# Order of the first loads, placement of the w_up casts, and the last down group and adds in a fused decoder layer

## The chip, the cores and the metric

The kernel runs on the 8 cores of one Trainium2 chip, each with its own part of the tokens. A time is device microseconds of the slowest core; the fast executions of one kernel differ by some 1 to 4 us. A second, slow state, with one die at a lower clock, appears now and then in any program on eight cores: here some executions of the kernel before (890 to 964 us) and of four variants (846 to 980 us).

Each execution also gives the span of every core. Their mean over the eight cores scatters by only about 0.3 us from one execution to the next (standard deviation), and it is used here beside the time, under the name **mean span**.

## The reference, cut to what matters

One decoder layer over 2,064 prompt positions for each of 8 sequences and 128 single tokens; widths 1,024 and 2,816.

```python
h = rmsnorm(x, g_pre_mix)
u, v, bg, cg, ga, gb = split(h @ w_in)             # w_in: 1024 x 4096
a = multiscale_pool(u, ..., w_pool, pool_scale)
b = (bg * causal_dwconv(cg * v)) @ w_conv_out
x = x + rmsnorm((sigmoid(ga) * a + sigmoid(gb) * b) @ w_o, g_post_mix)
h = rmsnorm(x, g_pre_ffn)
gate, val = split(causal_dwconv(h @ w_up))         # w_up: 1024 x 5632, as 44 blocks
y = (silu(gate) * val) @ w_down                    # 22 rows of blocks, 8 output groups
x = x + rmsnorm(y, g_post_ffn)
```

## The kernel before

Each core holds activations with channels on the 128 partitions. The mixer (up to the `w_o` product) runs over five token tiles of 512 or 392 columns, the FFN over six tiles of 344. Weights come as float32 and are cast to bf16 by the DMA on their way in; GpSimd issues these casts, and also the DMA that adds to its destination (`acc=True`). All instructions are first collected, then a list scheduler in the build fixes each engine's order. Loads can be tied to a point of the program by `after=[last_pe[0]]`: they are issued after that TensorE group.

TensorE's groups keep their order, except the short sums of the norms, which float: such a sum is placed when it has been ready for a set time (the patience, in nanoseconds) or when TensorE would stand still.

```python
# in the scheduler, for TensorE: c is the next fixed group, f the next floating sum
if c is None or ready[f.idx] + max(400.0, min(f.flt, f.pri - s - 4000.0)) <= s or sf <= s - 200.0:
    c, s = f, sf
```

The head. `xs0` are the five loads of the first x tile; SyncE issues them.

```python
wload(W_IN, w_in, 0)
warm(60)                                   # 60 small matmuls on a constant
for i in range(1, 16):
    wload(W_IN, w_in, i, after=[last_pe[0] if i < 3 else xs0[1]])
...                                        # w_pool, rest of w_in, w_co, then x1: after=[xs0[1]]
```

The 44 casts of `w_up` (256 KB in SBUF, 0.262 MB each) and the residual of tile 3, which accumulating transfers add:

```python
for i in range(16):                        # first half of the last mixer tile, L = 4
    F_block(L, i)
    wup(1)
    if i == 4:
        WO(L - 1)
        epi(L - 1)                         # tile 3: multiply, pool_dma(r, xs, acc=True), square, sums
...
for m in range(8):                         # second half: gates
    merge(t, m, *g[m])
    if t == L:
        wup(1)
...                                        # then one per w_o group, and one per FFN pair j of tile 0
if (t, j) in ((0, 9), (0, 11), ...):       # the 8 casts of w_down, from FFN pair 9 on
    wdn()
```

The end. A down group `m` is one chain of 22 matmuls over the gated rows `gb`; the last tile's eight groups follow the last pair directly. Then the norm, a multiply per row pair and the residual:

```python
pe([(bank(b, NB), wb[:, k, :], gb.ap[:, k, :]) for k in range(FC)], [W_DN.t(m, 1), gb.t()], [("ps", b)], NB)
...
steps = ((0, 2, None, "acc"), (2, 2, None, "pool"), (4, 2, 0, "dve"), (6, 2, 2, "dve"))
#         first row, rows, PSUM bank, who adds the residual: accumulating DMA, GpSimd, VectorE
```

## Time and profile before

| | kernel before |
|---|---|
| time, median before the change was tried | 822.18 us |
| profiled execution: cores | 817.4 to 820.1 us |
| mean span, 30 fast executions | 818.34 us |
| slowest core, mean of the same | 819.95 us |
| last matmul's start to the end, mean of 8 cores | 11.63 us |

The prediction below shows the page's first part, the waits of core 0 and its stall near 320 us. In these lines PE is TensorE, DVE VectorE, ACT ScalarE, POOL GpSimd and SP SyncE; L469 is the line of the kernel in which a helper issues every matmul. Core 0 is not typical, as only its clock fell after that stall, so here are core 1's stretches of TensorE from the timeline: start, duration, instruction group and count, and in brackets the idle time before the stretch and what the profile says ended it.

```profile
43.61 274.32 PE L469 MATMUL ps<-big 128*128 128x392 bf16 x1581 [0.54 <-DVE big L658]
319.42 6.13 PE L469 MATMUL ps<-big 128*128 128x392 bf16 x36 [1.49 <-DVE big L509]
326.08 80.32 PE L469 MATMUL ps<-big 128*128 128x392 bf16 x537 [0.52 <-ACT big L700]
407.26 371.37 PE L469 MATMUL ps<-big 128*128 128x346 bf16 x2536 [0.86 <-DVE big L821]
...
806.19 0.31 PE L469 MATMUL ps<-big 128*128 128x344 bf16 x1 [0.32 <-ACT big L848]
```

After 43.61 us TensorE stands still five times (the one left out here is the 0.69 us at 779 that the prediction discusses). Together that is 1.49 + 0.52 + 0.86 + 0.69 + 0.32 = 3.9 us in 763; everything else to be won lies before 43.61 and after 806.19.

The issue-to-landing view of the stretch from 285 to 420 us, core 0 (count, KB, median us from issue to landing):

```profile
big<-w_up POOLq DMA_DIRECT2D x38, 256.0 KB, 10.3
...
big<-xT POOLq DMA_DIRECT2D x4, 392.0 KB, 13.6
```

The last line is the four accumulates of tile 3.

### The profile page before, as it was taken

To read this page: it belongs to the slowest core of one execution; us is meant where nothing else is said; L and a number is where in the kernel's file an instruction comes from. 1 tells how busy PE (TensorE), PEld (TensorE's weight loads), DVE (VectorE), ACT (ScalarE), POOL (GpSimd) and SP (SyncE) were. 2 spreads that over 40 slices of the span, in tenths; PEclk is the share of its full clock that TensorE was granted. 3 is DMA by queue.
4 is the path that set the end of the run, shared out by engine and by line. 5 is a ranking of instruction groups with operands and counts; after the bars stand their busy time and mean duration, and the time that the engine had idled before them with its cause. 6 is when DMAs were issued, how large, how long until landed. Compare 5 with 4: busy or idle time off the path is not lost.

```text
span 820.1 us, 16719 instructions; the slowest of 8 cores (817.4 to 820.1 us)
## 1 busy us (share of the span) xinstructions
PE 798.2 (97%) x5118; PEld 498.9 (61%) x5118; DVE 563.4 (69%) x1054; ACT 450.7 (55%) x903; POOL 259.9 (32%) x296
## 2 busy tenths in 40 slices
PE   7999999999999998999999999999999999999994
PEld 5454455555555554666666666666666666666662
DVE  3896547877977595588986486568566765785722
ACT  3533375676475544686754475456556555765532
POOL 6542002002101261499532252225222522242221
PEclk9999999999999999999999999999999999999998
DMA  9999706567117799999960132015101500040063
GB/s 182 201 160 156 152 20 136 148 164 157 41 36 158 109 171 208 169 159 171 183 113 1 35 46 53 1 36 70 36 2 36 70 2 1 6 66 2 1 133 77
DMA packets 63735, 75.18 MB, mean 92 GB/s; under 512 B 3072, under 2 KB 59264, under 8 KB 63632
## 3 DMA queue, kind: packets, MB, share of 16 engines
q0 software_dynamic: 41440, 44.97, 38.9%
q1 hardware_dynamic: 22208, 29.14, 12.8%
q8 instruction: 44, 0.72, 0.3%
q14 instruction: 43, 0.35, 0.2%
HBM read 81.53 MB, written 22.90 MB: 127 GB/s over the span
## 4 chain that ended last, share of the span: by engine, by line
PE 90%; DMA 4%; DVE 2%; issue 2%; POOL 1%; ACT 1%; DVEq 0%; ACTq 0%; POOLq 0%
PE ps L469 90%; DMA big<-xT 4%; POOL big L482 1%; DVE big L549 0%; DVE big L783 0%; DVE big L821 0%; ACT big L520 0%; DVE big L509 0%; DVEq L1078 0%; DVE big L578 0%; ACT L520 0%; DVE big L658 0%; DVE big L867 0%; ACT big L848 0%; ACT big L768 0%
## 5 line engine op out<-in xcount | busy, mean ns | idle before, releaser
L469 PE MATMUL ps<-big 128*128 128x346 bf16 (+5 forms) x5118 | 798.2, 319 | 10.6 <-POOL big L922 2.9
L469 PEld LDWEIGHTS ps<-big 128*128 128x128 bf16 x5118 | 498.9, 98 | 309.6 <-issue 15.8
L821 DVE SCALAR_TENSOR_TENSOR big<-ps,big 128x344 f32<-128x344 f32 (+1 forms) x528 | 281.1, 569 | 94.8 <-ACT big L817 74.9
L835 POOL TENSOR_TENSOR big<-big 128x344 bf16<-128x344 f32 x132 | 125.5, 952 | 258.5 <-DVE big L821 186.2
L817 ACT ACTIVATE big<-ps,big 128x344 f32<-128x344 f32 (+1 forms) x264 | 139.4, 541 | 67.5 <-PE ps L469 61.7
L834 ACT ACTIVATE big<-big 128x344 f32<-128x344 f32 x132 | 64.6, 489 | 47.9 <-DVE big L821 45.9
L700 ACT ACTIVATE big<-ps 128x392 f32<-128x392 f32 (+1 forms) x80 | 38.9, 512 | 51.8 <-PE ps L469 34.7
L480 POOL DMA_DIRECT2D big<-xT x16 | 15.8, 997 | 153.4 <-DVE big L713 147.0
L845 ACT ACTIVATE big<-ps,big 128x344 f32<-128x344 f32 x48 | 26.0, 546 | 58.8 <-PE ps L469 55.8
L482 POOL DMA_DIRECT2D big<-w_up x44 | 33.3, 758 | 64.6 <-PE ps L469 52.8
L713 DVE SCALAR_TENSOR_TENSOR big<-ps,big 128x392 f32<-128x392 f32 (+1 forms) x40 | 25.8, 645 | 33.7 <-PE ps L469 31.4
L509 DVE TENSOR_TENSOR big<-big 128x1568 bf16<-128x1568 bf16 (+3 forms) x28 | 24.5, 875 | 32.2 <-ACT big L732 26.0
L851 DVE TENSOR_TENSOR big<-big 128x688 bf16<-128x688 bf16 x17 | 8.8, 518 | 41.5 <-ACT big L848 41.5
L480 POOL DMA_DIRECT2D yT<-big x21 | 27.3, 1523 | 31.0 <-DVE big L867 17.3
L730 ACT ACTIVATE big<-ps,big 128x392 f32<-128x392 f32 (+1 forms) x40 | 24.5, 613 | 13.0 <-PE ps L469 12.9
L606 DVE TENSOR_TENSOR big<-big 128x406 f32<-128x406 f32 (+7 forms) x50 | 29.8, 598 | 1.5 <-ACT big L628 0.2
L482 POOL DMA_DIRECT2D big<-w_in x32 | 23.2, 743 | 20.6 <-DMA big<-w_in 10.9
L575 ACT ACTIVATE big<-big 128x392 f32<-128x392 f32 (+1 forms) x20 | 12.7, 638 | 30.6 <-DVE big L664 30.5
L768 ACT ACTIVATE big<-big 128x784 bf16<-128x784 f32 (+1 forms) x20 | 17.8, 891 | 18.5 <-DMA big<-xT 16.0
L578 DVE SCALAR_TENSOR_TENSOR big<-big 128x392 f32<-128x392 f32 (+1 forms) x40 | 25.5, 644 | 3.6 <-ACT big L575 3.0
L848 ACT ACTIVATE big<-ps 128x344 bf16<-128x344 f32 x48 | 21.6, 451 | 10.4 <-PE ps L469 10.2
L719 DVE TENSOR_TENSOR big<-big 128x392 bf16<-128x392 f32 (+1 forms) x40 | 24.9, 631 | 2.3
(62 smaller groups left out, 353.4 us busy)
## 6 DMA issues: line engine op xcount, KB each, us to landing
big<-w_up POOLq DMA_DIRECT2D x44, 256.0 KB, 10.0
big<-w_in POOLq DMA_DIRECT2D x32, 256.0 KB, 22.6
yT<-big POOLq DMA_DIRECT2D x21, 344.0 KB, 6.2
big<-xT POOLq DMA_DIRECT2D x16, 392.0 KB, 8.9
yT<-big SPq DMA_DIRECT2D x8, 784.0 KB, 8.5
big<-w_dn POOLq DMA_DIRECT2D x8, 704.0 KB, 14.1
big<-xT SPq DMA_DIRECT2D x6, 784.0 KB, 6.2
big<-h2T SPq DMA_DIRECT2D x6, 692.0 KB, 5.8
```

The source lines that it names most:

```text
L469: ins = e.matmul(o, lhsT=l, rhs=x, start=(start and i == 0), stop=(stop and i == last))
L480: return S.add("pool", lambda e: e.dma_start(out=out, in_=in_, accum_op=ALU.add, max_dma_last_dim=mx), r, w, dma=True, byts=byts, pri=pri, ...
L482: return S.add("pool", lambda e: e.dma_start(out=out, in_=in_, max_dma_last_dim=mx), r, w, dma=True, byts=byts, pri=pri, after=after)
L578: dve(lambda e, k=k: e.scalar_tensor_tensor(out=cv, in0=p[:, 2 + k + lo:2 + k + N], scalar=cc(C_WC + 4 * k + c), in1=cv, op0=ALU.mult, op1 ...
L606: dve(lambda e, nx=nx, cur=cur, s=s, a2=a2: e.tensor_tensor(out=nx[:, a2:W], in0=cur[:, a2:W], in1=cur[:, a2 - s:W - s], op=ALU.add), [ct] ...
L700: act(lambda e, b=b, g=g: e.activation(out=GT[t].ap[:, g, lo:N], in_=bank(b, N, lo), func=AF.Sigmoid), [("ps", b)], [GT[t].t(g, 1)], N, ps ...
L713: dve(lambda e: e.scalar_tensor_tensor(out=A_, in0=bank(bp, N, lo), scalar=cc(C_PS + m), in1=A_, op0=ALU.mult, op1=ALU.mult), [("ps", bp), ...
L817: act(lambda e, b=b, fj=fj, tt=tt: e.activation(out=tt[:, 0:n], in_=bank(b, n), func=AF.Copy, scale=cc(C_WF + fj)), [("ps", b), KCST], [to ...
L821: dve(lambda e, b=b, fj=fj, tt=tt, k=k: e.scalar_tensor_tensor(out=tt[:, 0:n], in0=ps[:, b * 512 + k:b * 512 + k + n], scalar=cc(C_WF + 44 ...
L834: act(lambda e: e.activation(out=g, in_=g, func=AF.Silu), [T.t(0, 1)], [T.t(0, 1)], NB, tab="silu")
L835: S.add("pool", lambda e: e.tensor_tensor(out=gb.ap[:, j, :], in0=g, in1=v, op=ALU.mult), [T.t()], [gb.t(j, 1)], dur=NB * 2.17 + 100)
L845: act(lambda e: e.activation(out=Y.ap[:, m, :], in_=bank(b, NB), func=AF.Copy, scale=cc(C_G4 + m)), [("ps", b), KCST], [Y.t(m, 1)], NB, ps ...
```

## The change

The intent, part by part: (1) the first x tile is to come in alone before any weight; (2) fewer `w_up` casts are to stand before and among the accumulates, and the rest goes out two per gate pair; (3) floating sums wait longer for a natural gap, and the eight multiplies of `epi_x` are spread; (4) the first down group of the last tile is cut, so that it can start before the last two gated rows exist; (5) no accumulating DMA at the end: GpSimd adds rows 0 to 2, VectorE adds rows 3 to 7 from PSUM.

```diff
-  ... ready[f.idx] + max(400.0, min(f.flt, f.pri - s - 4000.0)) <= s ...
+  ... ready[f.idx] + max(1000.0, min(f.flt, f.pri - s - 4000.0)) <= s ...
@@ the down groups
-        pe([... for k in range(FC)], [W_DN.t(m, 1), gb.t()], [("ps", b)], NB)
+        for k0, k1 in ((0, 20), (20, 21), (21, 22)) if t == NTB - 1 and m == 0 else ((0, FC),):
+            pe([... for k in range(k0, k1)], [W_DN.t(m, 1), gb.t(k0, k1 - k0)],
+               [("ps", b)], NB, start=k0 == 0, stop=k1 == FC)
@@ the last adds
-            steps = ((0, 2, None, "acc"), (2, 2, None, "pool"), (4, 2, 0, "dve"), (6, 2, 2, "dve"))
+            steps = ((0, 2, None, "pool"), (2, 1, None, "pool"), (4, 2, 0, "dve"), (6, 2, 2, "dve"), (3, 1, 4, "dve"))
@@ the head
-    wload(W_IN, w_in, 0)
     warm(60)
-    for i in range(1, 16):
-        wload(W_IN, w_in, i, after=[last_pe[0] if i < 3 else xs0[1]])
+    for i in range(16):
+        wload(W_IN, w_in, i, after=[xs0[1 if i else 0]])
@@ the casts
             if t == L:
-                wup(1)
+                wup(2)
...
         F_block(L, i)
-        wup(1)
+        if i < 9:
+            wup(1)
@@ the multiplies of tile 4
-            if 20 <= 22 * t + j < 28:
-                epi_x(L, 22 * t + j - 20)
+            if 22 * t + j in EPX:            # (20, 21, 22, 23, 25, 26, 28, 29)
+                epi_x(L, EPX.index(22 * t + j))
@@ the residual's load for the end: all eight rows in place of rows 2 to 7
```

More of the change, by code (lines that the diff above doesn't have):

```diff
@@ L167, in order @@
                         sf = max(free[e], ready[f.idx])
-                        if c is None or ready[f.idx] + max(400.0, min(f.flt, f.pri - s - 4000.0)) <= s or sf <= s - 200.0:
+                        if c is None or ready[f.idx] + max(1000.0, min(f.flt, f.pri - s - 4000.0)) <= s or sf <= s - 200.0:
                             c, s = f, sf
@@ L841, in wdown @@
         wb = W_DN.ap[:, m, :].rearrange("p (k c) -> p k c", k=FC)
-        pe([(bank(b, NB), wb[:, k, :], gb.ap[:, k, :]) for k in range(FC)], [W_DN.t(m, 1), gb.t()], [("ps", b)], NB)
+        for k0, k1 in ((0, 20), (20, 21), (21, 22)) if t == NTB - 1 and m == 0 else ((0, FC),):
+            pe([(bank(b, NB), wb[:, k, :], gb.ap[:, k, :]) for k in range(k0, k1)], [W_DN.t(m, 1), gb.t(k0, k1 - k0)],
+               [("ps", b)], NB, start=k0 == 0, stop=k1 == FC)
         if mid:
@@ L872, in epi_y @@
                 yk, xk = Y.ap[:, k:k + n, :], X1.ap[:, k:k + n, :]
-                if how == "acc":
-                    pool_dma(yT[:, k:k + n, lo:lo + NB], yk, [Y.t(k, n)] + [("y", a, 0) for a in tiles_a(lo, lo + NB)],
-                             [("yo", t, k)], 2 * 128 * n * NB * 4, acc=True)
-                    continue
                 if how == "pool":
@@ L1030, in build_nc @@
     WD1 = {9: 0, 11: 1, 13: 2, 15: 3, 17: 4, 19: 5, 20: 6, 21: 7}
+    EPX = (20, 21, 22, 23, 25, 26, 28, 29)
     dn = [0]
@@ L1065, in build_nc @@
     lo = T0B + (NTB - 1) * NB
-    sp_dma(X1.ap[:, 2:8, :], yT[:, 2:8, lo:lo + NB], [("y", a, q) for a in tiles_a(lo, lo + NB) for q in range(2)],
-           [X1.t(2, 6)], 128 * 6 * NB * 4)
+    sp_dma(X1.ap, yT[:, :, lo:lo + NB], [("y", a, q) for a in tiles_a(lo, lo + NB) for q in range(2)],
+           [X1.t()], 128 * KC * NB * 4)
     for m in range(8):
```

## The prediction

> **What bounds the kernel now.** I read the page first, then the cores' spans, then the waits of TensorE, and last the timeline around each of its gaps. The page's first part, for the slowest core:
>
> ```profile
> span 820.1 us, 16719 instructions; the slowest of 8 cores (817.4 to 820.1 us)
> ## 1 busy us (share of the span) xinstructions
> PE 798.2 (97%) x5118; PEld 498.9 (61%) x5118; DVE 563.4 (69%) x1054; ACT 450.7 (55%) x903; POOL 259.9 (32%) x296
> ```
>
> TensorE does matmuls for 798.2 of 820.1 us; VectorE, next, has 69%. The change removes no matmul of the model, so all it can win is the other 21.9 us. The list of TensorE's waits says where half of that is:
>
> ```profile
> PE ps L469 <- POOL big L922: 2.9, 1, 2.9
> PE ps L469 <- DVE big L509: 2.3, 1, 2.3
> PE ps L469 <- ACT big L940: 1.8, 2, 1.1
> PE ps L469 <- DVE big L964: 1.1, 1, 1.1
> PE ps L469 <- ACT big L848: 1.0, 2, 0.7
> PE ps L469 <- DVE big L821: 0.9, 1, 0.9
> PE ps L469 <- DVE big L658: 0.5, 1, 0.5
> ```
>
> These sum to 10.5 us. The rest is the end: the last matmul is over at 808.76 us, and 11.3 us follow. So there are three places: the head (L922, L940, L964, L658), a stall in the middle (L509), and the end (L848 and the 11.3 us). The timeline of the middle:
>
> ```profile
> 292.97 0.96 POOL L480 DMA_DIRECT2D big<-xT  x1
> 293.56 1.11 POOL L482 DMA_DIRECT2D big<-w_up  x1
> ...
> 298.36 1.28 POOL L480 DMA_DIRECT2D big<-xT  x1
> ...
> 317.88 0.86 ACT L768 ACTIVATE big<-big 128x784 bf16<-128x784 f32 x1 [3.45 <-DMA big<-xT]
> ...
> 318.84 1.65 DVE L509 TENSOR_TENSOR big<-big 128x1568 bf16<-128x1568 bf16 x2 [3.96 <-ACT big L768]
> ...
> 320.63 4.61 PE L469 MATMUL ps<-big 128*128 128x392 bf16 x17 [2.29 <-DVE big L509]
> ```
>
> The residual of tile 3 is added by four accumulating transfers (big<-xT, line 480). They stand behind and between w_up casts (line 482) in GpSimd's queue. The last is issued at 298.36 and lands only near 317.8, 19.5 us later; tile 2's took a median of 6.5 us. Square, tree and the norm's sums follow, and TensorE, which has reached those sums at 318.34, stands for 2.29 us. On the other seven cores I read 0.85 to 1.84 us for it. Core 0 pays again: its clock falls, as this row of the stretches shows (busy times, then clock, DMA share, GB/s):
>
> ```profile
> 321.00:325.00 4.00, 4.00 (x16) 1.95 (x15) 1.93 (x5) 2.56 (x4) 0.00 (x0) 0.60 1.01 182
> ```
>
> **What the Trainium skill says.** (1) "TensorE: Matmul & The Clock Gate", "What's actually happening": the array runs at half clock after an idle window of about 3.4 us, and the windows run freely. The trace agrees in kind: 16 matmuls in 4 us where 26 fit on other cores, after a gap of only 2.29 us, so phase decides. (2) "DMA: Bandwidth & Descriptors", "Issuing engines are not separate DMA queues": SP's and GpSimd's transfers share 16 engines and interleave. It agrees: the accumulate took 6.5 us in light traffic and 19.5 behind casts. (3) "GPSIMD Engine Reference", "4.1 Engine selection": an add with two inputs is about twice as slow on GpSimd as on VectorE. Here 2.13 us (L878) stand against 0.87 (L882), 2.5 times.
>
> **The change part by part.**
>
> *Head.* The first weight block waits for the first piece of x0, the rest for the second; before, block 0 went out at 1.60 us and blocks 1 and 2 at 9.29, after the warm-up matmuls. This should bring x0 earlier by about 2 us. I do not believe that it comes out at the end. The chain has 12.74 us of the DMA that brings x1, issued at 14.39 behind weight blocks 1 to 7:
>
> ```profile
> 14.39 12.74 DMA big<-xT
> ...
> 29.53 7.14 PE ps L469 x42
> ```
>
> Between 13 and 23 us the engines already write 159 GB/s on average of ten rows of 1 us, which is one 0.262 MB cast in 1.65 us, and TensorE uses a block in 1.7 us (8 matmuls of 0.215). x0 (2.1 MB), eight blocks and x1 are the same bytes in another order. Only the low rows of 4 to 7 us (DMA share 0.72, 0.91, 0.70) can be filled: together 0.67 us. Estimate: 0.5 us won, between 0 and 1.5.
>
> *Casts of w_up.* In the first half of tile 4 nine go out in place of 16, then two per gate pair in place of one. In the built order the 9 now stand before all four accumulates, and none between them. The multiplies (L760) that release those start at 290.98, 292.87, 295.01 and 296.76 and take 0.97, so the last accumulate issues near 298 even so; with four casts ahead since 284 (4 x 1.65 = 6.6 us) and tile 2's 6.5 us to 9 us, it lands at 304.5 to 307. Square 0.86, tree 1.65 and 0.3 of hand-over give 307.5 to 310. The built order also moves those sums seven TensorE groups earlier (5.6 us), so TensorE gets there at 318.34 - 5.6 = 312.7: no stall. Worth per core: 0.85 to 1.84 us, and on core 0 2.29 plus some 1.5 of slow clock (10 of 26 matmuls, 0.16 us each), less 0.5, since the other cores show a 0.52 us wait for a sigmoid (L700) near 326 that core 0's slowness hid. With it removed, spans become 816.8, 815.9, 816.4, 817.3, 816.7, 817.0, 816.8 and 817.9: the slowest core falls by 2.2 us, from 820.1 to 817.9.
>
> *Sums' patience (400 to 1000 ns) and the spread of the eight multiplies of tile 4.* In the built order 103 FFN multiply-adds precede the first four L783 in both kernels, then 11, 1 and 1: no difference. The 0.9 us wait on L821 near 409 stays: 0.
>
> *Split of the last down group.*
>
> ```profile
> 780.31 0.91 POOL L835 TENSOR_TENSOR big<-big 128x344 bf16<-128x344 f32 x1 [1.13 <-DVE big L826]
> 780.99 0.46 ACT L848 ACTIVATE big<-ps 128x344 bf16<-128x344 f32 x1 [0.66 <-PE ps L469]
> ...
> 781.58 26.56 PE L469 MATMUL ps<-big 128*128 128x344 bf16 x181 [0.69 <-ACT big L848]
> ```
>
> The view blames L848, but the group does not read what that writes; it needs the 22 gated rows, and GpSimd ends the last at 781.22. After the split, 20 matmuls (2.9 us) run first, and row 21 is there before its turn. Worth 0.69 us, which the end inherits.
>
> *Last adds.* Rows 0 and 1 leave the accumulating DMA for GpSimd, row 3 goes to VectorE. VectorE from 810.06: multiplies of 2, 1, 2, 2 and 1 rows, then adds of 2, 2 and 1. A two-row one costs 0.83 in sequence, a one-row one about 0.48 (estimate: half the elements plus the same fixed part): 5 x 0.83 + 3 x 0.48 = 5.6 against 6 x 0.83 = 5.0, so VectorE ends 0.6 later, near 815.6. GpSimd: 2.13 + 1.1, done near 814.4. But the accumulate's extra read of 0.35 MB goes, and the first stores leave at 813.3 in place of 814.5. Before, the last store is issued at 815.5 and lands 4.4 later among the traffic; after, the last is a single row, 0.176 MB, issued near 815.8 with about 3 us to land. 818.9 against 819.9: 0.8 won, between -0.3 and 1.4.
>
> Sum: 0.5 + 2.2 + 0 + 0.69 + 0.8 = 4.2 us.
>
> **The rivals.** *Starved head*: TensorE starts sooner and waits for w_in. Core 7 already waits 0.7 us on w_in and core 6 1.6. Then the head gives 0, or loses 0.5: total 3.5. *Stall grows*: if the accumulates still landed at 317.8, the earlier sums would hold TensorE 317.8 + 2.8 - 312.7 = 7.9 us, and the time would be near 824. Against it: no cast stands between them now. *FFN weights late*: seven casts move behind 303 us. By 318 I count 21 issued before and 19 after; at the end of the gate pairs 24 and 25. The FFN starts near 342 with no wait on w_up before; two late casts are 3.3 us of stream, to be absorbed in 24 us. Were it to fail, it would cost 1 to 3 us: 819 to 821. *Longer end*: if the single row's store lands as slowly as before (4.4 us), the end loses 0.3: 819.
>
> **Range and chances.** The measured median of 822.18 stands 2.1 above the profiled span; I carry that over: 822.2 - 4.2 = 818.0 us. If core 0's slow clock is not in every run, less is won (820); if head and end both do their best, 4.2 + 1.0 + 0.6 = 5.8, and 816.4; with noise, 815.4. I take 815.4 to 820.6. Two per cent is 16.4 us, more than all that TensorE's waits hold, so within 2% is 0.97; slower 0.02, for a new stall with a cold clock; faster 0.01.
>
> **What would show it.** L509 gone from TensorE's waits and no stretch near 320 at a low clock (if L509 stays, the cast part is wrong); accumulates landing in under 10 us; no wait on big<-w_up; in the head, real matmuls start earlier but the x1 stage near 29.5 moves by under 1.5 us; the 0.69 wait at 781 gone; last matmul to end 10.5 us or less; L821's 0.9 still there. A wait on w_in of over 1 us or on w_up would make the number wrong, and so would a gain of the whole 2 us at the head.

## The result, and the profile after

| | before | after |
|---|---|---|
| time, median of 4 | 822.8 us | 818.2 us (816.92 to 818.84) |
| ratio of fast runs, 95% interval | | 0.9942 (0.9925 to 0.9960) |
| mean span | 818.34 us | 814.96 us |
| last matmul's start to the end, 8 cores | 11.63 us | 10.75 us |

Ratios are the mean time of one kernel's fast runs over that of the other's of the same rounds, so not quite the ratio of the medians. Executions in which one die ran at a lower clock are left out of the means. The change wins 0.6%, which is "within 2%". The mean span of the kernel before is that of the three later calls.

The page's first part, and core 1's stretches of TensorE after, against those above:

```profile
span 816.4 us, 16709 instructions; the slowest of 8 cores (813.3 to 816.4 us)
```

```profile
40.58 3.53 PE L469 MATMUL ps<-big 128*128 128x500 bf16 x16 [0.23 <-DVE big L658]
44.64 342.52 PE L469 MATMUL ps<-big 128*128 128x392 bf16 x2032 [0.53 <-DVE big L658]
388.69 415.69 PE L469 MATMUL ps<-big 128*128 128x346 bf16 x2839 [1.53 <-ACT big L817]
804.64 0.31 PE L469 MATMUL ps<-big 128*128 128x344 bf16 x1 [0.26 <-ACT big L850]
```

Read the starts first. The long stretch begins *later*, 44.64 against 43.61; over the eight cores the mean is 44.74 against 44.05. The waits at 319 (L509), 326 (L700) and 779 are gone. The 0.86 at 407 has gone too, but a longer one stands at 388.69. And there is a small new one at 40.58. The wait at 388 is seen on cores 0 to 4 (1.91, 1.53, 1.68, 1.98 and 0.80 us); cores 5 to 7 wait about 0.7 us near 405 in its place.

The issue-to-landing view of 285 to 420 us, core 0, after:

```profile
big<-w_up POOLq DMA_DIRECT2D x38, 256.0 KB, 19.7
...
big<-xT POOLq DMA_DIRECT2D x4, 392.0 KB, 5.8
```

The accumulates land in 5.8 us in place of 13.6, and the weights pay: a `w_up` block takes 19.7 us in place of 10.3. The transfers have not become slower: between 340 and 380 us core 0's moved 154 GB/s before and 153 after. The casts go out later and stand in a longer queue.

The end, core 0, first before, then after (SPq is SyncE issuing stores):

```profile
811.54 1.22 POOL L480 DMA_DIRECT2D yT<-big  x1 [17.28 <-DVE big L867]
812.30 2.13 POOL L878 TENSOR_TENSOR big<-big 128x688 f32<-128x688 f32 x1
813.19 1.65 DVE L882 TENSOR_TENSOR big<-ps,big 128x688 f32<-128x688 f32 x2
814.51 1.48 SPq L476 DMA_DIRECT2D yT<-big  x3
```

```profile
807.30 2.50 POOL L876 TENSOR_TENSOR big<-big 128x688 f32<-128x688 f32 x2 [16.74 <-DVE big L869]
807.48 2.08 DVE L869 TENSOR_TENSOR ps<-big,ps 128x688 f32<-128x688 f32 x3
809.01 3.10 SPq L476 DMA_DIRECT2D yT<-big  x5
809.47 2.07 DVE L880 TENSOR_TENSOR big<-ps,big 128x688 f32<-128x688 f32 x3
```

The last matmul started at 808.45 before and at 804.67 after. So SyncE's first store goes out 6.1 us after it before, and 4.3 us after it now. VectorE's adds begin at the same distance (4.7 and 4.8 us) and take 2.07 in place of 1.65 us.

### The profile page after: what moved, and what is told of

Read it like the earlier page. It is cut to its first block, busy times and chain, and to the rows that moved or that the text cites. A ratio compares the mean times of both kernels' runs of the same rounds, so it can differ in the third digit from the quotient of the medians.

```text
span 816.0 us, 16713 instructions; the slowest of 8 cores (813.3 to 816.4 us)
## 1 busy us (share of the span) xinstructions
PE 796.5 (98%) x5118; PEld 498.2 (61%) x5118; DVE 562.4 (69%) x1056; ACT 451.9 (55%) x903; POOL 258.7 (32%) x296
## 4 chain that ended last, share of the span: by engine, by line
PE 94%; DMA 2%; DVE 1%; issue 1%; ACT 1%; DVEq 0%; POOL 0%; SPq 0%; ACTq 0%; POOLq 0%
PE ps L469 94%; DMA big<-w_in 1%; DMA big<-xT 1%; DVE big L549 0%; DVE big L821 0%; ACT big L817 0%; POOL big L482 0%; DVEq L1077 0%; ACT big L958 0%; DVE big L658 0%; DVE ps L869 0%; SPq L476 0%; DVE big L869 0%; DVE big L880 0%; DVE big L664 0%
## 5 line engine op out<-in xcount | busy, mean ns | idle before, releaser
L469 PEld LDWEIGHTS ps<-big 128*128 128x128 bf16 x5118 | 498.2, 98 | 307.1 <-issue 12.9
L821 DVE SCALAR_TENSOR_TENSOR big<-ps,big 128x344 f32<-128x344 f32 (+1 forms) x528 | 281.1, 569 | 97.2 <-ACT big L817 75.1
L817 ACT ACTIVATE big<-ps,big 128x344 f32<-128x344 f32 (+1 forms) x264 | 140.1, 541 | 71.3 <-PE ps L469 67.1
L700 ACT ACTIVATE big<-ps 128x392 f32<-128x392 f32 (+1 forms) x80 | 39.3, 513 | 55.5 <-PE ps L469 35.8
L509 DVE TENSOR_TENSOR big<-big 128x1568 bf16<-128x1568 bf16 (+3 forms) x28 | 23.6, 847 | 30.8 <-ACT big L732 28.9
L730 ACT ACTIVATE big<-ps,big 128x392 f32<-128x392 f32 (+1 forms) x40 | 24.5, 611 | 13.6 <-PE ps L469 13.5
L480 POOL DMA_DIRECT2D yT<-big x20 | 26.2, 1550 | 12.9 <-DVE big L885 7.3
L850 ACT ACTIVATE big<-ps 128x344 bf16<-128x344 f32 x48 | 21.6, 450 | 13.5 <-PE ps L469 13.5
L549 DVE SCALAR_TENSOR_TENSOR big<-big 128x392 bf16<-128x392 f32 (+1 forms) x40 | 24.3, 647 | 5.9 <-ACT big L526 3.6
```

What stands on the lines that cost most here:

```text
L469: ins = e.matmul(o, lhsT=l, rhs=x, start=(start and i == 0), stop=(stop and i == last))
L480: return S.add("pool", lambda e: e.dma_start(out=out, in_=in_, accum_op=ALU.add, max_dma_last_dim=mx), r, w, dma=True, byts=byts, pri=pri, ...
L700: act(lambda e, b=b, g=g: e.activation(out=GT[t].ap[:, g, lo:N], in_=bank(b, N, lo), func=AF.Sigmoid), [("ps", b)], [GT[t].t(g, 1)], N, ps ...
L817: act(lambda e, b=b, fj=fj, tt=tt: e.activation(out=tt[:, 0:n], in_=bank(b, n), func=AF.Copy, scale=cc(C_WF + fj)), [("ps", b), KCST], [to ...
L821: dve(lambda e, b=b, fj=fj, tt=tt, k=k: e.scalar_tensor_tensor(out=tt[:, 0:n], in0=ps[:, b * 512 + k:b * 512 + k + n], scalar=cc(C_WF + 44 ...
```

## The experiments

Twelve kernels ran in three calls, each with its own runs of the kernel before (821.89, 821.6 and 821.88 us). All results were correct. The mean span of the kernel before was 818.30, 818.30 and 818.44. The standard error of a mean span is given where it decides; it is at most 0.3 us.

| run | what | median, us | ratio (95%) | mean span minus before |
|---|---|---|---|---|
| e1_head_only | part 1 alone, patience 400 | 821.0 | 0.9992 (0.998 to 1.0003) | -0.5 |
| e2_casts_only | part 2 alone | 821.35 (fast runs) | 0.9987 (0.9969 to 1.0006) | -1.7 |
| e3_split_only | part 4 alone | 820.81 | 0.9992 (0.998 to 1.0004) | -0.8 |
| e4_tail_only | part 5 alone | 821.65 | 0.9991 (0.9979 to 1.0003) | -0.8 |
| e5_after_oldhead | all but part 1 | 817.42 | 0.9946 (0.9933 to 0.996) | -3.9 |
| e6_after_wdn10 | after, first w_down cast later | 818.37 (fast runs) | 0.9957 (0.994 to 0.9975) | -3.3 |
| e7_after_12casts | after, 12 casts for 9 | 817.27 | 0.9941 (0.9929 to 0.9953) | -3.9 |
| e8_combo1 | e5 and e6 together | 816.79 (fast runs) | 0.994 (0.9927 to 0.9953) | -4.1 |
| e9_12casts_again | e7 again | 817.07 | 0.9943 (0.9929 to 0.9957) | -4.2 |
| e10_12casts_oldhead | e9, old head | 815.77 (fast runs) | 0.9928 (0.9914 to 0.9942) | -5.1 |
| e11_12casts_w0early | e9, weight block 0 early | 816.85 | 0.9945 (0.9926 to 0.9964) | -4.1 |
| e12_12casts_patience400 | e9, patience 400 | 816.25 | 0.9934 (0.992 to 0.9948) | -5.3 |

After itself: -3.4. The time alone would have told little of e1 to e4, whose intervals all reach 1; the mean spans tell more.

### The parts alone: e1 to e4

The edits are the hunks of the diff above, each applied alone to the kernel before: "the head", "the casts", "the down groups" (with the patience left at 400 in all four), and "the last adds" with the residual's load.

> The kernel before with only the head of the change (weight block 0 waits for the first piece of x0, blocks 1 to 15 for the second). Starved head (what the trace after suggests): block 0 lands only near 14 us, TensorE waits 1.4 to 2.4 us on big<-w_in before its first weight group, the first piece of x1 comes about 0.5 us later, and the time is 0.5 to 1 us longer than before. The prediction's estimate: 0.5 us shorter. Either way x0's last piece should be in about 1.5 us earlier.

> The kernel before with only the casts moved (nine in tile 4's first half, two per gate pair). Theory: the accumulates land in under 10 us and the wait on L509 near 318 is gone (worth 1 to 2.3 us on TensorE), but the last w_up block now lands late, so a new wait of 1.5 to 2 us appears on most cores near 388 in place of the 0.9 near 409; in sum 1 to 3 us shorter than before. Rival (the prediction: no late w_up): 2.2 us shorter with no new wait near 388.

> The kernel before with only the last down group 0 split at rows 20 and 21. Theory: the 0.69 us wait near 781, which the view puts down to L848, was for GpSimd's last gated row; it disappears and the time is 0.7 us shorter. Rival: the view is right that it is ScalarE's L848; then the wait stays and the time is the same.

> The kernel before with only the last adds changed (rows 0 to 2 added by GpSimd, row 3 by VectorE in PSUM, no accumulating store). Theory: the stretch from the last matmul's start to the end falls from 11.65 us to about 10.7, the time by 0.9. Rival: VectorE's own longer chain eats it, and the time is the same within 0.3.

*Head alone:* faster by 0.5 us in the mean span (817.81 with a standard error of 0.18, against 818.30). The loss that the trace of after had made me expect did not come. TensorE's waits on VectorE L658 are absent on all eight cores of this run. The waits on `w_in` came as expected (1.6 to 2.2 us on cores 0, 2 and 5), and still the kernel did not become slower.

*Casts alone:* the stall at 320 is gone on all eight cores, and so is the L700 wait. The mean span falls by 1.7 us, but the slowest core only from 819.97 to 819.12. Cores 0 and 6 of the profiled execution show why. First core 0's stretch, then its stretch by windows (busy times with counts, then clock, DMA share and GB/s), then the same window on core 1, which did not wait there so long:

```profile
389.33 2.12 PE L469 MATMUL ps<-big 128*128 128x346 bf16 x10 [2.60 <-DMA big<-w_up]
```

```profile
391.00:395.00 4.00, 4.00 (x20) 2.28 (x19) 1.72 (x4) 1.67 (x4) 1.86 (x2) 0.66 1.16 263
```

```profile
391.00:395.00 4.00, 4.00 (x30) 2.67 (x28) 4.00 (x8) 2.62 (x6) 1.42 (x3) 1.00 1.17 266
```

Here the profile names the culprit of the wait near 388: the DMA of a `w_up` block. Cores 1, 5 and 7 of this run wait there too (0.33, 0.82 and 0.18 us), so five cores of eight, though only two by the 1.5 us or more that was expected on most. On these three, and in after, the same wait bears the names L821, L817 or L509, whichever semaphore came last by the profile. That it is the same can be read from the landing of the last `w_up` block: in e2, after and e5, which issues these casts as after does, fourteen cores wait near 388, and on each of them TensorE goes on 0.34 or 0.35 us after that block has landed. The wait costs core 0 2.60 us and then ten matmuls' worth of slow clock (20 in 4 us against 30), and core 6 likewise (3.05 us, 18 matmuls). Their spans are 819.8 and 820.4 us, those of the other six 815.1 to 816.5.

*Split alone:* the 0.69 us wait at 779 is gone on all cores, and the mean span falls by 0.8. *Last adds alone:* from the last matmul's start to the end it takes 10.84 us (mean of 8 cores) in place of 11.63, and the mean span falls by 0.8. Each is what was predicted (0.69 and 0.8).

### Old head, later w_down, more casts: e5 to e8

```diff
e5:  the hunk "the head" undone in after
e6:  - if (t, j) in ((0, 9), (0, 11), ...): wdn()      + if (t, j) in ((0, 10), (0, 11), ...): wdn()
e7:  - if i < 9: wup(1)                                + if i < 12: wup(1)
e8:  e5 and e6 together
```

> The changed kernel with the head of the kernel before. If the new head costs 0.5 to 1 us, this is that much faster than the changed kernel: ratio to before near 0.993 where the changed kernel had 0.9942. If the head is worth nothing, 0.9942 again.

> The changed kernel with one transfer order swapped: the first w_dn cast (1.44 MB read) is issued after the last w_up cast instead of before it. Theory (the new wait of 1.5 to 2 us near 388 on cores 0 to 3 is for the last w_up block, behind that w_dn cast): the last w_up block lands about 4 us earlier, the wait near 388 is gone on all cores, a wait on L821 of 0.7 us near 405 comes back, and the time is about 1 us shorter than the changed kernel. Rival (VectorE is late there, as the view says, L821 or L817): the wait near 388 stays at 1.5 to 2 us.

> The changed kernel with 12 casts in tile 4's first half in place of 9 (two per gate pair as there). Theory: three more casts stand before the accumulates, 3 x 1.65 us, so the last accumulate lands 3 to 5 us later than in the changed kernel; TensorE's sums, which the order puts three groups later (3 us), meet it with a wait of 0 to 1 us on L509; the last w_up block in turn lands 3 to 5 us earlier and the wait near 388 is gone. In sum the same as the changed kernel or up to 1 us shorter. Rival: no wait either way, and 1 us shorter.

> The changed kernel with both repairs: the head of the kernel before, and the first w_dn cast after the last w_up cast. If both theories hold, their gains add: about 1.5 to 2 us shorter than the changed kernel, near 816.4 us, ratio to before near 0.992.

The wait at 388 is settled by e6. In after, the last `w_up` cast goes out behind the first cast of `w_down`, which is 2.75 times as large; in e6 it goes out ahead of it. GpSimd's issues, core 0, after and then e6:

```profile
360.58 0.76 POOL L482 DMA_DIRECT2D big<-w_up  x1
361.33 0.90 POOL L482 DMA_DIRECT2D big<-w_dn  x1
363.13 0.74 POOL L482 DMA_DIRECT2D big<-w_up  x1
```

```profile
362.94 0.76 POOL L482 DMA_DIRECT2D big<-w_up  x1
363.69 0.91 POOL L482 DMA_DIRECT2D big<-w_dn  x1
```

The last block is issued at about the same time (363.13 and 362.94). The issue-to-landing view of that one cast, core 0 (after in the window from 363 to 364 us, then e6 from 362.5 to 363.3):

```profile
big<-w_up POOLq DMA_DIRECT2D x1, 256.0 KB, 25.2
```

```profile
big<-w_up POOLq DMA_DIRECT2D x1, 256.0 KB, 18.0
```

So it lands near 388.4 in after and near 380.9 in e6, and no core of e6 nor of e8 waits near 388, 16 of 16. This fits what the Trainium skill says ("DMA: Bandwidth & Descriptors", section "Two DMAs through the same engine are not ordered"): within one queue of one DMA engine, descriptors start in order. All 16 cores then wait 0.7 us near 405, as cores 5 to 7 of after did. So the wait there is another one, which the longer wait had hidden. In the mean the waits near 388 and 405 fall only from 1.25 to 0.70 us, and the mean spans do not show even that: e6 815.02 against after 814.96, e8 814.25 against e5 814.39. Within the profiled executions it can be seen: from the start of the stretch near 44 us to the last matmul's start it takes 759.18 us in e6 and 759.72 in after (means of 8 cores), but e6's stretch began 0.7 later. The cause of the wait is shown, a gain in time is not; the 1 us expected of e6 and the 1.5 to 2 us of e8 did not come.

In e7, with three more casts ahead of the accumulates and still none among them, these take 9.3 to 10.6 us in place of 5.8 to 6.9, and still no core stalls near 312. The wait near 388 is gone, and that near 405 shrinks to 0.2 us or nothing. The mean span falls by 0.6 us to 814.39 (standard error 0.15). So nine was too few: 12 casts keep the gain at 320 and do not pay for it at 388. They are not quite free. On 7 of the 40 cores profiled with twelve casts (e7, e9, e10, e11, e12) TensorE waits 0.3 to 1.1 us between 311 and 338 us, for ScalarE L700 or for the load of `h2T`; with nine (after, e5, e6, e8) none of 32 does.

e5 raised a doubt about the head: old head 814.39 (standard error 0.23), new head 814.96 (0.13), while the head alone had won 0.5. The times do not show it (ratios 0.9946 and 0.9942), and after ran in another call.

### What the head costs, and why: e9 to e12

```diff
e9:   e7 again
e10:  the hunk "the head" undone
e11:  - wload(W_IN, w_in, i, after=[xs0[1 if i else 0]])
      + wload(W_IN, w_in, i, after=[xs0[1] if i else ms])     # ms: GpSimd's second memset
e12:  - max(1000.0, ...                                       + max(400.0, ...
```

> The kernel after with twelve casts in the first half of tile 4 (in place of nine), run again as the partner of the three that follow; they differ from it in one thing each. Both theories: 817.3 us in the median (e7 gave 817.27), ratio to before 0.994, no wait of over 0.3 us between 50 us and the last down groups on any core.

> Twelve casts, and the old head (weight block 0 first, blocks 1 and 2 behind the warm-up). Theory 'the new head loses': over 24 profiled cores the long stretch of TensorE began at 44.9 us with the new head and at 44.1 with the old one, so this kernel ends 0.8 us before its partner, near 816.5 us, with the stretch at about 44.1. Rival 'the head is neutral' (the head alone left the first accumulate at 293.0 as before, and the time at 0.9992): within 0.3 us of the partner.

> Twelve casts, new head, but weight block 0 is sent right after the first fills, as before; blocks 1 to 15 still wait for the second piece of x0. Theory 'block 0 late' (TensorE waits 1.4 to 2.4 us on w_in near 14.4 because block 0 goes out only at 5.3 to 7): that wait goes and the long stretch begins at about 44.1, as with the old head; time near 816.5. Rival 'x1 late' (x1 is sent at 14.0 behind the same bytes, and its landing decides): the wait on w_in goes, but the stretch still begins near 44.7, and the time is the partner's.

> Twelve casts, the rest of the change, but the sums' patience back at 400 ns. The prediction put the patience at 0: time within 0.3 us of the partner. Rival 'the patience costs in the head' (the head alone with 400 was neutral, the same head with 1000 began the stretch 0.8 us later): the first accumulate goes out about 1 us earlier than in the partner, and the time is near 816.3.

e9 repeats e7 (mean span 814.26 and 814.39), but its expectation that no core would wait over 0.3 us in the long stretch failed: core 2 waits 0.57 us for L700 and core 6 0.32 for `h2T`. e9 and e10 differ by 0.96 us in the mean span (814.26 and 813.30, each with a standard error of 0.14) and by 1.3 in the median: the new head loses, in this company. e9 and e12 differ by 1.10 (813.16, 0.13) and 0.8: the patience loses as much. So with the old patience the new head is harmless, and e10 and e12 are equal within their errors (the old head with the old patience and twelve casts was not run). Core 0 around 40 us, e9 and then e12:

```profile
40.43 3.53 PE L469 MATMUL ps<-big 128*128 128x500 bf16 x16 [0.23 <-DVE big L658]
...
44.49 0.82 PE L469 MATMUL ps<-big 128*128 128x392 bf16 x4 [0.53 <-DVE big L658]
```

```profile
37.21 8.06 PE L469 MATMUL ps<-big 128*128 128x392 bf16 x39
```

The built orders explain most of the difference between e9 and e12. Before, the first floating sum, that of tile 1's norm, is TensorE's group 30 (counted from 0). With the new head and patience 400 it moves one group earlier, to 29 (e1, e12); VectorE's L658 then comes in time, and no core of e1 or e12 waits for it. With patience 1000 the sum is back at 30 (after, e5, e9, e10), and TensorE waits 0.53 us near 44, as before, and on the new head 0.23 more near 40 on nearly every core. These waits are 0.76 us of the 1.10. The profiles agree: from the first matmul on x1 to the first accumulate of tile 3 it takes 263.7 us in e9 and 262.9 in e12 (means of 8 cores). That accumulate goes out at 293.3 us in both, and not 1 us earlier in e12 as expected: e12's profiled execution reached x1 at 30.43 us, e9's at 29.63, and four of e12's cores had less than the full clock in the head. For the other 0.3 the errors are too large. One more floating sum moves with the patience, tile 2's near 264 us; there two cores of e12 wait 0.22 and 0.46 us, and none of e9 does.

Rival "block 0 late" fell with e11. With block 0 sent early the long stretch begins at 45.01 us (mean of 8 cores), no earlier than in e9 (44.41), and the mean span is that of e9. Waits on `w_in` remained on six of eight cores, so not block 0 alone is late; and what block 0 won, x0 lost: block 0 landed at 13.5 us in place of 14.0, x0's last piece at 14.0 in place of 12.9 (means).

What the new head does to the stream, as the mean of GB/s over the eight cores, read from the windows of every core:

| kernel | 5 to 10 us | 10 to 15 us | 0 to 30 us |
|---|---|---|---|
| before | 223 | 209 | 202 |
| after | 243 | 183 | 201 |
| e10 (old head) | 216 | 213 | 202 |
| e9 (new head) | 237 | 186 | 201 |

x0 comes earlier by what the row of 5 to 10 us carries more, and in the next 5 us as much is missing. By 30 us the same bytes have moved. TensorE cannot use the earlier x0, as its first weight block now goes out behind x0's first piece and comes later. Two pieces of after's chain of waits, slowest core (start, duration, what):

```profile
5.85 8.15 DMA big<-w_in
...
14.13 1.95 PE ps L469 x6
```

The block is issued at 5.85, lands at 14.00, and the first matmul with a weight block starts at 14.13. In the mean over the eight cores x0's last piece lands at 12.82 us in place of 14.05, the first weight block at 13.99 in place of 12.82, and the first matmul with a weight block starts at 14.16 in place of 14.03: the new head exchanges one wait for the other. There may be a second cost. Having done its warm-up matmuls earlier, TensorE waits 1 to 3 us for `w_in` and is caught at half clock more often: between 10 and 20 us the granted clock was under 1 on 13 of the 56 cores profiled with the new head (seven kernels), and on 3 of 56 with the old one. The 13 lie in four kernels (after, e1, e6 and e12), and e9 has none. Where it hits, it hurts. e6's core 5 waited 2.73 us, and its 66 matmuls of the first tile took 16.80 us where after's core 0 took 14.21; its long stretch began at 47.16 us.

Where the 0.96 us between e9 and e10 go is thus not shown. Their profiled executions differ by only 0.18 us of mean span (813.89 and 813.71), and both have the full clock on all cores between 10 and 20 us. The clock over all fast executions gives a hint: its mean is lower with the new head in each of the four pairs (e1 0.9945 against before 0.9949, after 0.9952 against e5 0.9953, e6 0.9950 against e8 0.9955, e9 0.9952 against e10 0.9956). 0.0004 of 815 us is 0.3 us, an estimate that leaves most of the 0.96 open.

The best versions are e10 (815.77 us) and e12 (816.25 us). They beat before by 0.7%, and e9, the partner, by 1.0 and 1.1 us of mean span; e9 itself stands 0.7 below after, of another call.

## Why the prediction was right or wrong

The time was right: 818.0 predicted, 818.2 measured. By its steps, in mean spans:

| step | predicted | measured |
|---|---|---|
| head | -0.5 | -0.5 alone (e1); +0.6 to +1.0 in the full change (e5, e10) |
| casts, mean of the cores | -1.65 (818.5 to 816.85) | -1.7 (e2) |
| casts, slowest core | -2.2 | -0.85 (e2) |
| patience and spread | 0 | +1.1 with the new head (e12) |
| split | -0.69 | -0.8 (e3) |
| last adds | -0.8 | -0.8 (e4) |

- **The casts part was right in its mechanism.** The last square of tile 3 started at 305.5 to 309.1 us over the cores of after, and the last accumulate landed at 305.4 to 309.0, against the predicted 304.5 to 307. That is later than predicted on six cores, by up to 2 us, but with the 2.8 us that follow still ahead of the sums' place near 312.7; TensorE did not stall there, and core 0's slow clock near 321 did not come. The "stall grows" rival is out.
- **Wrong, the 0.52 us wait on L700.** The prediction took 0.5 off because it would remain on all cores. It vanished on all eight. With twelve casts it is back on five cores of 40 (0.29 to 1.00 us).
- **Wrong, the dismissal of "FFN weights late".** I counted that at the end of the gate pairs nearly as many `w_up` casts are out as before (24 and 25) and let the queue behind absorb the rest. But the count of issues is not the landing: a block took 19.7 us to land in place of 10.3, and the last block, behind a large `w_down` cast, held TensorE on five of eight cores (25.2 us from issue to landing, core 0). The prediction also looked for the wait under the name "w_up"; in after it carries three other names. Its size was inside what the prediction would have charged (1 to 3 us), and in the mean it replaced the 0.9 us wait of L821 near 408 with 1.25.
- **The step that failed is the zero for the patience.** The prediction says that "103 FFN multiply-adds precede the first four L783 in both kernels, then 11, 1 and 1: no difference". That was looked up only where the patience was meant to act, near 409 us. It acts in the head, where one sum moves by one group, and that costs 0.76 of the 1.10 us. The spread of the eight multiplies is indeed nothing: built without it, every engine's order is the same.
- **The head was right alone, and probably for another reason.** "The same bytes in another order" was right in the stream: after 5 to 10 us had carried more, 10 to 15 us carried less. But its sign "real matmuls start earlier" failed, with 14.16 us against 14.03 for the first weight block. What e1 won is more likely the 0.54 us wait that the moved sum removes, which the prediction never considered. In the full change the patience takes that back, and "starved head" came true: waits on `w_in` of 0.4 to 2.4 us on all cores. The prediction had said that such a wait of over 1 us would make its number wrong. It came on six cores, and the number held: luck.
- **Three readings of hardware were off.** That GpSimd's add takes 2.5 times VectorE's was read in the kernel before, where it began while GpSimd was still issuing the accumulating store (811.54 to 812.76 us, the lines of the end above). In after the same add takes 1.63 us against 0.87, 1.9 times, so GpSimd is done sooner than the 2.13 + 1.1 us reckoned; why it took longer before is not shown. And the slow clock after a gap of 2.29 us does not follow from an idle window of 3.4 us; the prediction let the two agree "in kind". Its point (2) is on transfers of different issuers, but GpSimd issues both the accumulates and the casts, so the stall is no test of it. The head is: with the new order SyncE's x0 landed 1.2 us earlier and GpSimd's first weight block 1.2 us later.
- **The split and the end were right**, also in saying that the label L848 was wrong: the cut makes the wait vanish without touching what L848 writes.

So part of the agreement is luck: an unforeseen loss of about 1 us near the head and a wait near 388 stand against an L700 wait that went away. The single parts sum to -3.8 us and the whole gives -3.4; with the patience's loss they would give -2.7. The rest of 0.7 us is hardly more than the error of such a sum (about 0.6 us, from the standard errors of its terms), so it says nothing of how the parts act together.

## What to carry to other kernels

Thinning a queue ahead of an urgent transfer makes everything behind it later: look for the last item of the displaced stream and what large transfer it now stands behind, and search for its wait by place, as the label may name another engine. A scheduler's constant has to be checked over the whole built order, not only where it was meant to act. When parts are worth under 1 us on several cores, compare the mean of the cores' spans, and treat a long gap on TensorE as a risk to its clock besides its length (here no gap up to 2.03 us lowered it, and four of the five of 2.29 us and more did).

## What the Trainium skill lacked or had wrong

- "TensorE: Matmul & The Clock Gate", "What's actually happening", gives an idle window of about 3.4 us. Here shorter gaps sufficed. Of TensorE's gaps after 50 us in the fourteen profiled executions (8 cores each), the sixteen of 1.42 to 2.03 us left the clock of the next 4 us at 1.00. Of the five longer ones, 2.29 us lowered it once (before, core 0: 0.65) and once not (e5, core 0: 1.00), and 2.60, 3.05 and 4.35 us lowered it to 0.62, 0.57 and 0.63 (e2, cores 0 and 6; e3, core 0).
- "DMA: Bandwidth & Descriptors" has no figure for what a backlog of casts does to a transfer behind it. Here an accumulate of 392 KB took 5.8 us (core 0, median of four) with four casts issued in the 9 us ahead of it (after), 9.3 with seven ahead (e7), and 13.6 with seven ahead and four among them (before); a 256 KB cast took 10.3 or 19.7.
- "GPSIMD Engine Reference", "4.1 Engine selection", has an add with two inputs about twice as slow on GpSimd, and this holds (1.63 us in after against 0.87 on VectorE, which read one input from PSUM). It has no figure for an add that begins while GpSimd still issues a transfer: there the same add took 2.13 us (before).
- "Perfetto Trace Analysis", "Optimization Strategy", advises to find the gap and the semaphore that blocks it. It does not warn that the last of several can name the wrong engine: in the view used here one and the same wait was put down to `w_up` in e2 and to L821, L817 and L509 in after, each time 0.35 us after the same cast had landed.
- No page sets a transfer's place in one queue against its size: a 256 KB cast behind a 704 KB one made five cores of eight wait 0.8 to 2.0 us, and none when the two changed places.
